# Own gate blocks of the second RG-LRU layer as three products of split parts, with the second parts made by GpSimd

## The chip, the core and the metric

One core of a Trainium2 chip runs the whole program. The time is the device time in microseconds (us) of one execution; a kernel's time is the median of several runs. The engines are TensorE (PE in the profile; PEld is its weight load), VectorE (DVE), ScalarE (ACT), GpSimd (POOL) and SyncE (SP), which here only issues DMAs. Each engine runs its own instructions in order and waits for others by semaphores.

## The reference

A trunk of four layers on 256 tokens of width 1024 in float32: an RG-LRU mixer, a gating mixer, a short convolution, and an RG-LRU mixer again, each followed by a squared-ReLU MLP. The change touches the last mixer, the second RG-LRU layer:

```python
gate, xr = jnp.split(h @ w_in, 2, axis=-1)          # 1024 -> 2 x 1280
gate = jax.nn.gelu(gate)
xr = _causal_dwconv(xr, conv_w) + conv_b            # 4 taps
xh = xr.reshape(b, s, A_HEADS, A_HEAD_DIM)          # 16 heads of 80
r  = sigmoid(einsum("bshi,hij->bshj", xh, gate_a_w) + gate_a_b)
ig = sigmoid(einsum("bshi,hij->bshj", xh, gate_x_w) + gate_x_b)
log_a = -LRU_C * r * softplus(-lam)
a = exp(log_a);  u = sqrt(-expm1(2 * log_a)) * (ig * xr)
hs = associative_scan(a, u)
return (hs * gate) @ w_out                          # 1280 -> 1024
```

## The kernel before

**Products.** TensorE computes most products of float32 values as three products of split parts: both operands are split into a rounded first part (type float32r) and the rest, and `mm3` (L251) adds first x first, first x second and second x first. Weights are split on the core: a chunk of 128 x 2048 arrives in two halves of 1024 columns (`raw`), ACT makes the first part of each half (`whi`, L187) and DVE the rest (`wlo`, L190). There are 12 raw buffers (`rawp`, L136) and five buffers each for `whi` and `wlo` (L137, L138). `next_chunk` (L236) keeps chunks asked for up to four ahead. SP issues each load as soon as a raw buffer is free.

**Gates.** The 1280 channels are ten tiles of 128 channels, in two groups of five. They are ordered so that four tiles of a group hold one whole head and part of another, and the fifth (the hub) the remaining parts. The gate matrices of a group are thus an own block of 128 x 128 for each of the five tiles and each of the two gates, four row strips from the hub to the others (L756) and four column strips back (L763). They come in two raw chunks of eight and six blocks, which are not split: `gate_steps` (L728) multiplies them as plain float32 (L748, L756, L763). A tile's products of both gates fill one PSUM bank of eight.

**Order of the work.** TensorE's instructions run in the order in which the program writes them. For the layer they are a generator (`tensor_steps`, L674) whose steps are mostly twelve products each. In this layer (`LRU_ORDER[1]`) steps 1 to 20 project the convolution branch (ten tiles), 21 to 24 are the first gates, 25 to 28 two gated tiles, 29 to 32 the second gates, 33 to 48 the other eight gated tiles, 49 to 68 the output projection, four steps for each pair of hidden tiles.

What the other engines do between is written out by hand in `LRU_STEPS[1]` (L73 to L77) and read by `run` (L646). `P` or `P2` lets the generator go on by one step or two. `C` is the next cast of a raw half on ACT, `S` the next split on DVE. Every other word is a method with a tile or pair number, and `in_order` (L203) ties each instruction behind the one before it on its engine, so the list is each engine's order. The words that matter here, by pair of tiles unless said:

- `ns`, `na`, `nv`: the row of the norm (ACT, TensorE, ACT and DVE).
- `x`: branch bank times that row (DVE, L794). `K`: last tap and bias (ACT, L802, two instructions). `k`: the other three taps (DVE, L808, six instructions). Their result is the tile pair `xc`.
- `wE`: loads ACT's table for the exponential (L869). `r` (by tile): both tanh of a tile's gates (ACT, L820), which frees its bank. `e`: decay terms (ACT, L832). `d`, `u`, `v`, `w`, `a`, `z`: the rest of the recurrence and the scan (DVE). `s`: square root (ACT, L846).
- `g`, `G`: gated bank times the row (DVE, L873), gelu (ACT, L877). `m`: scan times gate (DVE). `i`, `o`: the first and second part of the hidden pair for the output projection (ACT L885, DVE L890).

Of the kernel before, what the change touches and what calls it, by code (L numbers as in the profile page):

```python
# [9 lines left out]
F32 = mybir.dt.float32  # L10
F32R = mybir.dt.float32r
# [4 lines left out]
P = 128  # L16
T = 256
D = 1024
KD = D // P
# [7 lines left out]
CHUNK = 2048  # L27
# [25 lines left out]
LRU_ORDER = (  # L53
    (
        ("branch", 8), ("branch", 2), ("gated", 4), ("gates", 0),
        ("gates", 1), ("gated", 2), ("gated", 4),
    ),
    (
        ("branch", 4), ("branch", 2), ("branch", 4), ("gates", 0),
        ("gated", 2), ("gates", 1), ("gated", 4), ("gated", 4),  # L60
    ),
# [16 lines left out]
)  # L78


# [12 lines left out]
ROW_LAYERS = (1,)  # L93

UNSPLIT = None


def _const_columns():
# [15 lines left out]
def trunk(ctx: ExitStack, tc: tile.TileContext, xT, consts, sbias, first, weights, out, widths, whole, causal):  # L114
    nc = tc.nc
    MULT, ADD, SUB, MAX = ALU.mult, ALU.add, ALU.subtract, ALU.max
# [7 lines left out]
    def pool(name, n_bytes, at=None, bufs=1):  # L124


        nonlocal taken
        gap = 0 if at is None else (at - taken) % 1024
        if gap:
            ctx.enter_context(tc.tile_pool(name=f"before_{name}", bufs=1)).tile([P, gap // 4], F32, name=f"gap_{name}")  # L130
        taken += gap + n_bytes
        return ctx.enter_context(tc.tile_pool(name=name, bufs=bufs))
# [3 lines left out]
    rawp = pool("rawp", 12 * 4096, 0, bufs=12)  # L136
# [4 lines left out]
    def wtile(dtype=F32, name="wk"):  # L141
        return wide.tile([P, 2, T], dtype, name=name, tag="wk", bufs=N_WIDE)

    def bank():
        return psum.tile([P, 512], F32, name="ps", tag="ps")
# [4 lines left out]
    ready = {}  # L150
# [44 lines left out]
    used = [0]  # L195
# [24 lines left out]
    def ask():  # L220
        with tc.high_priority(offset=-LATER):
            for load, cast, split in fetch(asked[0]):
                load()
                casts.append(cast)
                splits.append(split)
            asked[0] += 1
            if not placed[0]:
                make_parts()

    def make_parts():  # L230
        while splits:
            if casts and len(casts) == len(splits):
                casts.pop(0)()
            splits.pop(0)()

    def next_chunk():  # L236
        i = used[0]
        used[0] += 1
        while asked[0] < n_chunks:
            ahead = sum(n not in whole for n in range(i + 1, asked[0]))  # L240
            if asked[0] > i and ahead + (asked[0] not in whole) > AHEAD:
                break
            ask()
        return ready.pop(i)
# [385 lines left out]
    class Mixer:  # L630


        def __init__(self, layer, nxt):
            self.layer = layer
            self.nxt = nxt
            self.added = False
            self.sq = {}
            self.scale = RowScale() if layer in ROW_LAYERS else Scales()
            self.banks = {"branch": [], "gated": [], "gates": {}}
            self.xr, self.xc, self.hs, self.gs, self.parts = {}, {}, {}, {}, {}  # L640
            self.rg, self.ig, self.qs, self.t = {}, {}, {}, {}
            self.acc = None
            self.in_order = chain()
            self.tensor = self.tensor_steps()
# [29 lines left out]
        def tensor_steps(self):  # L674
# [32 lines left out]
            for i in range(KR // 2):  # L707
                whole_pair = (self.layer, i) == UNSPLIT
                if whole_pair:
# [18 lines left out]
        def gate_steps(self, g):  # L728

            at, w = 0, None

            def block():
                nonlocal at, w
                if at % 8 == 0:
                    w = next_chunk().rearrange("p (k w) -> p k w", w=P)
                at += 1
                return w[:, (at - 1) % 8, :]

            hub = g * GRP + GRP - 1
            tiles = range(g * GRP, hub)
            banks = self.banks["gates"]

            for m in (*tiles, hub):
                banks[m] = bank().rearrange("p (j t) -> p j t", t=T)
                for e in range(2):
                    nc.tensor.matmul(banks[m][:, e, :], block(), self.tile_of(m), start=e == 0, stop=False,  # L748
                                     skip_group_check=True)
                if m in (tiles[1], hub):  # L750
                    yield
            for e in range(2):
                b = block()
                for i, m in enumerate(tiles):
                    q = slice(i * SHARE, (i + 1) * SHARE)
                    nc.tensor.matmul(banks[m][:, e, :], b[q], self.tile_of(hub)[q], start=False, stop=True,  # L756
                                     tile_position=(i * SHARE, 0), skip_group_check=True)
            yield
            for e in range(2):
                b = block()  # L760
                for i, m in enumerate(tiles):
                    q = slice(i * SHARE, (i + 1) * SHARE)
                    nc.tensor.matmul(banks[hub][q, e, :], b[:, q], self.tile_of(m), start=False, stop=True,  # L763
                                     tile_position=(0, i * SHARE), skip_group_check=True)
            yield
# [40 lines left out]
        def k(self, i):  # L806
            c, x = self.xc[i], self.xr[i]
            return [nc.vector.scalar_tensor_tensor(out=c[:, j, d:], in0=x[:, j, :T - d],  # L808
                                                   scalar=self.tap(3 - d, 2 * i + j), in1=c[:, j, d:],
                                                   op0=MULT, op1=ADD)  # L810
                    for d in (1, 2, 3) for j in range(2)]


        def r(self, m):
# [292 lines left out]
    for step in HEAD_STEPS.split():  # L1107
        what, i = step[0], int(step[1:] or 0)
# [39 lines left out]
def _out_chunks(w):  # L1148
    return [w[k:k + 2 * P].reshape(2, P, D).transpose(1, 0, 2).reshape(P, 2 * D) for k in range(0, w.shape[0], 2 * P)]
# [32 lines left out]
def _weight_chunks(p):  # L1182
# [7 lines left out]
    for i, kind in enumerate(KINDS):  # L1190
        j = counts[kind]
        counts[kind] += 1
        if kind == "a":
# [8 lines left out]
            for n, c in enumerate(_out_chunks(p["a_w_out"][j])):  # L1202
                out += unsplit([c[:, :D], c[:, D:]]) if (j, n) == UNSPLIT else [c]
        elif kind == "b":
# [63 lines left out]
```

## Time and profile before

| | |
|---|---|
| median of 3 runs | 1063.13 us (1063.07 to 1063.28) |
| the profiled execution | 1063.05 us, of which its span is 1061.3 us |
| PE, PEld busy | 1053.5 us (99%), 1041.9 us (98%) |
| DVE, ACT busy | 716.4 us (68%), 615.5 us (58%) |
| POOL busy | 27.2 us (3%) |
| granted clock of TensorE | 0.998 of full speed |

A row of the timeline has start and duration in us, the engine, the line, the operation, out<-in by the program's names (buffer numbers left out), shapes and count, and in brackets how long the engine stood idle before it and what ended that. Rows of equal instructions that follow each other are merged. A plain float32 product has two records on TensorE, so ten of them are "x20". In the second RG-LRU layer the branch projection ends and the first gates begin at 809.72 us, the second gates run from 821.75 to 828.14 us.

### The profile page before, as it was taken

The numbers are of one execution on the slowest core, as the hardware profiler recorded it, in microseconds if no ns is written. First come the engines' busy times: TensorE is split into PE (matmuls) and PEld (weight loads), VectorE is DVE, ScalarE is ACT, GpSimd is POOL, SyncE is SP. The second block draws the span as 40 slices with busy tenths as digits, with TensorE's granted clock in tenths as the row PEclk, the third lists the DMA queues.
The fourth block names the chain that finished last, engine by engine and source line by source line (L and its number), as shares of the span: only waits on it lengthen the run. The fifth ranks groups of instructions, "written<-read, shape, count | busy, mean of one in ns | idle before, by whom it ended". The sixth has DMA issues, their size and how long they took to land.

```text
span 1061.3 us, 21619 instructions
## 1 busy us (share of the span) xinstructions
PE 1053.5 (99%) x9138; PEld 1041.9 (98%) x9138; DVE 716.4 (68%) x921; ACT 615.5 (58%) x866; POOL 27.2 (3%) x75
## 2 busy tenths in 40 slices
PE   9999999999999999999999999999999999999997
PEld 9999999999899999999999999999999999999997
DVE  7999965565758754545797764455589899655553
ACT  7798644454664754445554574446556977544442
POOL 2400000000110000000000000000000000000000
PEclk9999999999999999999999999999999999999999
DMA  9655676555556566555475466555645546755301
GB/s 339 254 236 179 235 262 199 196 188 197 196 170 207 189 208 200 196 187 185 153 237 196 159 228 206 190 191 179 196 152 180 186 149 222 259 197 191 129 1 40
DMA packets 58417, 203.39 MB, mean 192 GB/s; under 512 B 6608, under 2 KB 7760, under 8 KB 58320
## 3 DMA queue, kind: packets, MB, share of 16 engines
q1 hardware_dynamic: 58176, 201.75, 56.2%
q8 instruction: 71, 1.16, 0.4%
q10 hardware_dynamic: 144, 0.26, 0.1%
q14 instruction: 26, 0.21, 0.1%
HBM read 200.94 MB, written 1.05 MB: 190 GB/s over the span
## 4 chain that ended last, share of the span: by engine, by line
PE 99%; DVE 0%; DVEq 0%; issue 0%
PE ps L253 92%; PE ps L937 2%; PE ps L748 2%; PE ps L699 1%; PE ps L756 0%; PE ps L259 0%; PE ps L763 0%; PE ps L973 0%; PE ps L695 0%; PE ps L1047 0%; PE ps L1054 0%; PE ps L393 0%; DVE o L1071 0%; PE ps L337 0%; DVEq L1264 0%; PE ps L422 0%
## 5 line engine op out<-in xcount | busy, mean ns | idle before, releaser
L190 DVE TENSOR_TENSOR wlo<-raw,whi 128x1024 fp32r<-128x1024 f32 (+1 forms) x379 | 442.9, 1199 | 225.9 <-ACT whi L187 225.9
L253 PE MATMUL ps<-xs,whi 128*128 128x256 f32 x3120 | 533.3, 276 | 0.0
L187 ACT CAST whi<-raw 128x1024 fp32r<-128x1024 f32 (+1 forms) x379 | 375.7, 1030 | 266.7 <-issue 153.4
L253 PEld LDWEIGHTS ps<-xs,whi 128*128 128x128 f32 x3120 | 469.9, 188 | 1.3 <-issue 0.4
L253 PE MATMUL ps<-xs,wlo 128*128 128x256 f32 x1560 | 430.7, 276 | 0.0
L253 PE MATMUL ps<-lo,whi 128*128 128x256 f32 x1312 | 362.2, 276 | 0.0
L253 PE MATMUL ps<-hi,wlo 128*128 128x256 f32 x1312 | 362.1, 276 | 0.0
L253 PE MATMUL ps<-hi,whi 128*128 128x256 f32 x1312 | 362.1, 276 | 0.0
L253 PEld LDWEIGHTS ps<-xs,wlo 128*128 128x128 f32 x1560 | 292.9, 188 | 0.0
L253 PEld LDWEIGHTS ps<-lo,whi 128*128 128x128 f32 x1312 | 246.3, 188 | 0.1
L253 PEld LDWEIGHTS ps<-hi,whi 128*128 128x128 f32 x1312 | 246.3, 188 | 0.0
L253 PEld LDWEIGHTS ps<-hi,wlo 128*128 128x128 f32 x1312 | 246.3, 188 | 0.0
L530 DVE TENSOR_TENSOR lo<-hsq,hi 128x512 fp32r<-128x512 f32 x64 | 44.0, 688 | 52.6 <-ACT hsq L528 51.3
L527 ACT ACTIVATE hi<-u 128x512 fp32r<-128x512 f32 x64 | 40.3, 630 | 24.3 <-DVE u L526 23.8
L291 ACT ACTIVATE xs<-x,cst 128x256 fp32r<-128x256 f32 x64 | 29.2, 502 | 31.1 <-DVE x L478 28.6
L524 ACT ACTIVATE u<-ps 128x512 f32<-128x512 f32 x32 | 18.9, 592 | 48.2 <-PE ps L253 48.2
L528 ACT ACTIVATE hsq<-u 128x512 f32<-128x512 f32 x64 | 39.5, 617 | 0.0
L295 DVE SCALAR_TENSOR_TENSOR xs<-x,cst,xs 128x256 fp32r<-128x256 f32 x64 | 28.6, 482 | 8.4 <-ACT xs L291 8.4
L526 DVE SCALAR_TENSOR_TENSOR u<-ps,rs 128x512 f32<-128x512 f32 x32 | 22.0, 687 | 16.8 <-PE ps L253 16.6
L808 DVE SCALAR_TENSOR_TENSOR xc<-xr,cst,xc 128x255 f32<-128x255 f32 (+2 forms) x60 | 24.1, 475 | 0.0
L315 DVE TENSOR_TENSOR sum<-sum,sq 128x256 f32<-128x256 f32 x52 | 21.9, 420 | 1.3 <-ACT sq L496 0.6
L937 PE MATMUL ps<-whi,xs 128*128 128x512 f32 x64 | 20.5, 394 | 0.0
(150 smaller groups left out, 479.4 us busy)
## 6 DMA issues: line engine op xcount, KB each, us to landing
raw<-weights SPq DMA_DIRECT2D x369, 512.0 KB, 4.2
raw<-first SPq DMA_DIRECT2D x16, 256.0 KB, 4.3
raw<-weights SPq DMA_DIRECT2D x4, 384.0 KB, 6.6
x<-xT SPq DMA_DIRECT2D x8, 128.0 KB, 4.0
out<-o SPq DMA_DIRECT2D x3, 256.0 KB, 2.7
sb<-sbias SPq DMA_DIRECT2D x2, 256.0 KB, 5.3
out<-o ACTq DMA_DIRECT2D x1, 256.0 KB, 3.4
cst<-consts SPq DMA_DIRECT2D x1, 128.0 KB, 6.5
```

The lines of the kernel that those rows point to most:

```text
L187: return nc.scalar.copy(out=hi[:, s], in_=raw[:, e])
L190: return nc.vector.tensor_tensor(out=lo[:, s], in0=raw[:, e], in1=hi.bitcast(F32)[:, s], op=SUB)
L253: nc.tensor.matmul(ps, a, b, start=start and n == 0, stop=stop and n == 2, skip_group_check=True)
L291: return nc.scalar.activation(xs_now[k][0], x_res[k // 2][:, k % 2, :], AF.Copy, scale=col(g_name, g_at + k))
L295: return nc.vector.scalar_tensor_tensor(out=lo, in0=x_res[k // 2][:, k % 2, :], scalar=col(g_name, g_at + k), in1=hi.bitcast(F32), op0=MUL ...
L315: return [nc.vector.tensor_tensor(out=sq_now[0], in0=sq_now[0], in1=sq[:, j, :], op=ADD) for j in range(2)]
L526: yield nc.vector.scalar_tensor_tensor(out=u, in0=ps, scalar=0.0, in1=both(scale.row), op0=MAX, op1=MULT)
L527: yield nc.scalar.activation(hi, u, AF.Square)
L528: yield nc.scalar.activation(sq, u, AF.Square)
L530: yield nc.vector.tensor_tensor(out=lo, in0=sq, in1=hi.bitcast(F32), op=SUB)
L808: return [nc.vector.scalar_tensor_tensor(out=c[:, j, d:], in0=x[:, j, :T - d], scalar=self.tap(3 - d, 2 * i + j), in1=c[:, j, d:], op0=MUL ...
L937: nc.tensor.matmul(ps[c], xs[a][:, s], b[:, k, :], start=kk == 0 and n == 0, stop=kk == KD - 1 and n == 2)
```

## The change

In the second RG-LRU layer (`SPLIT_GATES = (1,)`), the own blocks of the four tiles beside the hub are multiplied as three products of split parts. The hub's own blocks and all strips stay plain products. New steps make the parts:

- `W` casts the first gate chunk (eight blocks, 1024 columns) on ACT into a buffer `ghi`, and `V` makes the second part `glo` on GpSimd. Both buffers come from the 12 of `rawp`. `W` waits until the chunk has been asked for.
- `B` casts one or two tiles of `xc` on ACT into `xh`, and `N` makes the second parts `xl` on GpSimd. `B0.1` stands for tiles 0 and 1; group 0 takes `B0.1`, `B2.3`, group 1 `B5`, `B6.7`, `B8`.

The generator has as many steps as before: the first step of a group now holds all products with `xh` (16), the second those with `xl` (8) and the hub's two plain ones. The list of steps changes up to `r3`; from there it is the same.

```diff
-    "P4 C P C P ns S C S P na nv S C P S x0 x1 K0 K1 P2 C P S C k0 P S C x2 K2 k1 P S C P k2 P S P wE P C P C P2 "
-    "x3 x4 K3 K4 S k3 P P k4 P2 r3 r1 P r0 P C S P S e0 P u0 P g0 r2 C u1 P d0 e1 S r4 P d1 C P r8 S P r9 C u4 P "
+    "P4 C P C P ns S C S P na nv C P x0 x1 K0 K1 W0 V0 P2 C P k0 P x2 K2 k1 B0.1 N0.1 C S P S B2.3 N2.3 C P S k2 "
+    "C B5 N5 P S P C wE W1 V1 P C P C S P2 x3 x4 K3 K4 S k3 P P B6.7 N6.7 k4 P B8 N8 S P r3 r1 P r0 P C S P S e0 "
+    "P u0 P g0 r2 C u1 P d0 e1 S r4 P d1 C P r8 S P r9 C u4 P e4 S P2 d4 P s0 s1 v0 P v1 w0 G0 a0 P w1 r5 z0 C P "
...
@@ gate_steps
-            for m in (*tiles, hub):
+            split = self.layer in SPLIT_GATES
+            if split:
+                next_chunk()
+                at = 8
+                for m in tiles:
+                    banks[m] = bank().rearrange("p (j t) -> p j t", t=T)
+                for part, x in enumerate((self.xh, self.xl)):
+                    for i, m in enumerate(tiles):
+                        for e in range(2):
+                            for n, w in enumerate(self.gw[g][:2 - part]):
+                                nc.tensor.matmul(banks[m][:, e, :], w[:, 2 * i + e, :], x[m],
+                                                 start=e == 0 and part == 0 and n == 0, stop=False,
+                                                 skip_group_check=True)
+                    if part == 0:
+                        yield
+            for m in (hub,) if split else (*tiles, hub):
@@ new steps
+        def W(self, g):
...
+            while i not in ready:
+                ask()
+            raw = ready[i]
+            hi = rawp.tile([P, 1024], F32R, name="ghi", tag="raw")
+            lo = rawp.tile([P, 1024], F32R, name="glo", tag="raw")
+            self.gw[g] = [t.rearrange("p (k w) -> p k w", w=P) for t in (hi, lo)]
+            self.gate_parts = (raw, hi, lo)
+            return nc.scalar.copy(out=hi, in_=raw)
+
+        def V(self, g):
+            raw, hi, lo = self.gate_parts
+            return nc.gpsimd.tensor_tensor(out=lo, in0=raw, in1=hi.bitcast(F32), op=SUB)
+
+        def B(self, *ms):
+            n = len(ms)
+            hi = self.xh_new = wtile(F32R, "xh")[:, :n, :]
...
+            return nc.scalar.copy(out=hi, in_=self.xc[ms[0] // 2][:, j:j + n, :])
+
+        def N(self, *ms):
+            n = len(ms)
+            lo = wtile(F32R, "xl")[:, :n, :]
...
+            return nc.gpsimd.tensor_tensor(out=lo, in0=self.xc[ms[0] // 2][:, j:j + n, :],
+                                           in1=self.xh_new.bitcast(F32), op=SUB)
```

Before `x3`, the new list has 11 `C` and 7 `S` where the old one has 10 and 8; up to `r3` both have 9 `S`.

More of the change, by code (lines that the diff above doesn't have):

```diff
@@ L95 @@
 UNSPLIT = None
+SPLIT_GATES = (1,)
 def _const_columns():
@@ L637, in __init__ @@
             self.sq = {}
+            self.first_chunk = used[0]
+            self.gw, self.xh, self.xl = {}, {}, {}
             self.scale = RowScale() if layer in ROW_LAYERS else Scales()
@@ L811, in k @@
                     for d in (1, 2, 3) for j in range(2)]
+        def W(self, g):
+            i = self.first_chunk
+            for what, arg in LRU_ORDER[self.layer]:
+                if what == "gates":
+                    if arg == g:
+                        break
+                    i += 2
+                else:
+                    i += arg * P * KD // CHUNK
+            while i not in ready:
[12 more added lines that the diff above has]
+            hi = self.xh_new = wtile(F32R, "xh")[:, :n, :]
+            j = ms[0] % 2
+            for d, m in enumerate(ms):
+                self.xh[m] = hi[:, d, :]
+            return nc.scalar.copy(out=hi, in_=self.xc[ms[0] // 2][:, j:j + n, :])
+        def N(self, *ms):
+            n = len(ms)
+            lo = wtile(F32R, "xl")[:, :n, :]
+            j = ms[0] % 2
+            for d, m in enumerate(ms):
+                self.xl[m] = lo[:, d, :]
+            return nc.gpsimd.tensor_tensor(out=lo, in0=self.xc[ms[0] // 2][:, j:j + n, :],
+                                           in1=self.xh_new.bitcast(F32), op=SUB)
         def r(self, m):
```

6 rows, old and new, of the table LRU_STEPS are left out of this document.

## The prediction

> **What bounds the kernel now.** I read the page first, then the chain of work in order of time around the second RG-LRU layer, then the timelines of ScalarE (ACT), VectorE (DVE), the DMA queue (SPq) and GpSimd (POOL) there.
>
> ```profile
> span 1061.3 us, 21619 instructions
> PE 99%; DVE 0%; DVEq 0%; issue 0%
> ```
>
> TensorE is the bound: 99% of the chain that ended last is PE. In the layer the chain has no piece that is not PE:
>
> ```profile
> 792.01 17.71 PE ps L253 x156
> 809.72 4.32 PE ps L748 x20
> ...
> 816.11 5.64 PE ps L253 x48
> ...
> 828.14 58.69 PE ps L253 x516
> ...
> 887.07 164.59 PE ps L253 x1452
> ```
>
> Columns: start, duration, engine and line, count. L748 is the own gate blocks (ten products a group, two records each), L253 the split products. So the change can gain on PE only what it takes out of L748, and it loses whatever its new waits put between PE's steps. One profiled execution took 1063.05 us against a median of 1063.13; its span is 1061.3, and what lies around the span I leave as it is. All sums below start from 1063.05. A difference under 0.2% (2.1 us) is about what a measurement of this kernel cannot tell from none.
>
> **What the products gain.** A plain product costs 4.32 / 10 = 0.432 us; a split one 164.59 / 1452 = 0.1134, three of them 0.340. The change swaps 4 tiles x 2 gates x 2 groups = 16 blocks: 16 x (0.432 - 0.340) = 1.47 us less on PE, 0.74 in each group. Bounds: each new product loads its own weights as every L253 product does, so I see no reason for another pitch. If nothing else happened: 1061.6.
>
> **What the step lists add to ACT.** These are the rows of the layer:
>
> ```profile
> 798.66 2.08 ACT L802 ACTIVATE xc<-xr,cst 128x256 f32<-128x256 f32 x4 [4.93 <-DVE xr L794]
> ...
> 809.13 1.28 ACT L869 ACT_TABLE_LOAD   x1
> ...
> 816.66 0.46 ACT L820 ACTIVATE rg<-ps,half_b 128x256 f32<-128x256 f32 x1
> ...
> 866.39 2.01 ACT L187 CAST whi<-raw 128x1024 fp32r<-128x1024 f32 x2 [0.74 <-PE ps L253]
> 868.31 0.61 ACT L885 CAST hi<-rg 128x512 fp32r<-128x512 f32 x1
> ...
> 871.83 2.00 ACT L187 CAST whi<-raw 128x1024 fp32r<-128x1024 f32 x2 [2.92 <-issue]
> ```
> ```profile
> 795.67 2.35 DVE L190 TENSOR_TENSOR wlo<-raw,whi 128x1024 fp32r<-128x1024 f32 x2
> 797.94 1.28 DVE L794 TENSOR_TENSOR xr<-ps,rs 128x512 f32<-128x512 f32 x2
> ...
> 816.29 4.81 DVE L808 SCALAR_TENSOR_TENSOR xc<-xr,cst,xc 128x255 f32<-128x255 f32 x12
> ...
> 857.51 0.69 DVE L890 TENSOR_TENSOR lo<-rg,hi 128x512 fp32r<-128x512 f32 x1
> ...
> 868.95 0.69 DVE L890 TENSOR_TENSOR lo<-rg,hi 128x512 fp32r<-128x512 f32 x1
> ```
>
> ACT gets W0, W1 (a 128x1024 cast each, 0.95 us at the pitch of the 2.00 us pair) and B0.1, B2.3, B6.7 (128x512 casts, 0.61 as L885 at 868.31, 0.53 at pitch) and B5, B8 (one tile each, 0.4 between that and half of it). The list also has one C more ahead of `x3` (11 against 10) and the same number after it. So from there on every C takes the raw half after the one it took before.
>
> *First wait: the last hidden tile behind one C too many.* A step P is 12 products, 1.36 us. P49 starts at 828.14 + 16 x 1.36 = 849.90, P65 at 871.67. The row at 871.83 is the cast of the chunk five after the one that P61 to P64 use: there are five `whi` buffers, so it stood idle 2.92 us and began 0.16 after P64 ended. Before, `i4` (868.31) and `o4` (868.95) lay ahead of that cast. In the changed list `C S C P m4 S P i4 o4` the second C is that cast, so `i4` queues behind a wait for P64, and P65 needs `i4` and `o4`. Price: 0.16 + 0.95 + 0.61 + 0.69 = 2.4 us of idle PE, whatever happened earlier. I find no cover for it.
>
> *Second wait: the gates' tanh behind the last convolution.* `B6.7` and `B8` stand ahead of `r3 r1 r0` on ACT and `B8` needs `k4`, while before `r3` (816.66) ran beside `k3 k4` (816.29 to 821.1). When does `k4` end? The two splits ahead of `x0 x1` are put off (2.27 at their pitch), so `x0` starts at 795.67, K0 at about 796.4, `k0` at 797.5. Behind it on DVE: k0 2.4 (half of the 4.81 at 816.29), x2 0.60, k1 2.4, three S 3.4, k2 2.4, to 808.7. Then ACT sets the time: B5 0.4, C 0.95, table 1.28 and `wE` 0.1, W1 0.95, two C 1.9, K3 1.0 (half of 2.08) end at 815.3, and `k3 k4` (4.81) at 820.1. `B8` 0.4: `r3` at 820.5, 3.85 later than before. ACT has no slack to win that back:
>
> ```profile
> 822.00:850.00 28.00, 28.00 (x244) 26.30 (x243) 24.92 (x36) 27.47 (x47) 0.00 (x0) 1.00 0.54 186
> ```
>
> The fourth busy figure is ACT's: 27.47 of 28 us. I let 0.6 of the 3.85 be absorbed, so the third hidden tile's `o2` (857.51) comes 3.2 later, at 861.4 with its 0.69. PE wants it at P57, 860.78 before, 859.3 with the gain: 2.1 us. I take 2.0, bounds 0 (if `k4` ends two us sooner) to 3.
>
> Sum so far: 1063.05 - 1.47 + 2.4 + 2.0 = 1066.0.
>
> *Third wait: a raw buffer for W0.* `ghi` and `glo` come from the 12 raw buffers that the weight stream uses.
>
> ```profile
> 796.95 0.33 SPq L184 DMA_DIRECT2D raw<-weights  x1
> ```
> ```profile
> 798.05 0.33 SPq L184 DMA_DIRECT2D raw<-weights  x1
> ```
> ```profile
> SPq L184 <- DVE wlo L190: 77.7, 22, 11.6
> ```
>
> Start, duration, queue and line; the last row is the queue's waits by what ended them (total, times, longest). The DMAs at 796.95 and 798.05 went out just as the two splits at 795.67 ended (796.9 and 798.0): a freed buffer is taken at once, all twelve are in use, and the queue's waits are all for a split. The change puts those two splits behind `k1`, so the first buffer to come free after `K1` does so at 797.5 + 2.4 + 0.6 + 2.4 + 1.2 = 804.1. W0, ready at 798.4, waits for that if the stream has taken every earlier one; queued behind it on ACT are a C, K2, B0.1 and so on to K3. K2 then starts at 806.0, and from there K2 1.0, B0.1 0.53, C 0.95, B2.3 0.53, two C 1.9, B5 0.4, C 0.95, `wE` and its table 1.4, W1 0.95, two C 1.9 and K3 1.0 end at 817.5; W1 waits for a buffer of its own, which I put at 0.7. So K3 ends at 818.2, 2.9 later, and `r3` starts at 823.4. This reaches PE in full: of eight PSUM banks the gates of the first group hold five and a gated bank one, so the second group finds two, and its third and fourth tile wait for those that `r3` and `r1` free. Price 2.9, bounds 0 and 4.
>
> Free in this change: POOL's queue (the same row has POOL at 0.00, so nothing else stands behind V and N), the chunk that W asks for (it has been fetched by then), the other moved splits (the half at 795.67 is first used at P25, 816.1), and the later DMAs (the transfer of 796.95 becomes 805 to 810, its cast is at 816).
>
> **What GpSimd costs.** The trace has no two-input operation of this width on POOL. Nearest rows:
>
> ```profile
> 265.57 1.10 POOL L1079 TENSOR_SCALAR_AFFINE_SELECT raw<-raw 128x1024 f32<-128x1024 f32 x1 [225.17 <-DMA raw<-weights]
> ...
> 285.16 1.13 POOL L321 TENSOR_SCALAR rc<-rc 128x2 int32<-128x2 int32 x1 [18.50 <-ACT rc L320]
> 286.38 0.19 POOL L324 TENSOR_TENSOR rc<-rc 128x2 f32<-128x2 f32 x1
> ```
> ```profile
> 266.42 2.46 DVE L190 TENSOR_TENSOR wlo<-raw,whi 128x1024 fp32r<-128x1024 f32 x2 [3.08 <-ACT whi L187]
> ...
> 283.89 2.35 DVE L190 TENSOR_TENSOR wlo<-raw,whi 128x1024 fp32r<-128x1024 f32 x2
> ```
>
> One input of 1024 columns takes 1.10, so V takes 1.1 to 2.2 and N half of that for two tiles; I take the upper end, one pass for each input. At that, V0 from about 806 ends by 809.7, where P21 begins: it is hidden, but only just. The second pair of rows shows contention: an operation on two numbers, else 0.19, took 1.13 at 285.16 and ended as the splits ended (286.24), and in the other order the splits at 266.42 took 2.46 instead of 2.35 where they met the end of the POOL operation. So the two engines shut each other out at least partly. I price that in the forecast at nothing and carry the rest as a rival. For the duration, the Trainium skill, "GPSIMD Engine Reference", section 3.1, gives 4497 ns for a two-input sum of 2048 columns; an estimate from that page for V is 2.25 us and the sum would stay the same. No run so far shows it.
>
> **Forecast.** 1063.05 - 1.47 + 2.4 + 2.0 + 2.9 = 1068.9 us.
>
> **The rivals.**
>
> *No wait reaches PE (the other side).* It needs a `whi` buffer for the extra C before P64 ends, and `o2` no more than 1.1 us later than before. For: PE had no idle piece in the layer, and `o4` was 2.0 us early. Against: the row at 871.83 shows that very cast waiting for P64. It gives 1061.6. It decides at P65: if PE's step there follows without a gap, this is it. Chance 0.07.
>
> *Only the last wait.* W0 has its buffer and `k4` ends by 818, so `r3` is less than 2 us late and P57 loses nothing: 1061.6 + 2.4 = 1064.0. For: DVE's own work up to `k4` sums to some 22 us from 795.7, which would end it at 817.5. Against: K3 waits on ACT. Chance 0.10.
>
> *No wait for a raw buffer.* 1066.0. For: the program's order of buffers is not in the trace of before, and W0's operands have long landed. Chance 0.25.
>
> *DVE shut out by GpSimd.* Every N and V blocks the convolutions for its whole time: V0, N0.1, N2.3 and N5 hold back `k2` and its followers by 2.2 + 1.1 + 1.1 + 0.55 = 4.95, of which 1.3 is the time that `B5` had to spare on ACT, and N6.7 holds back `k4` by 1.1: 4.7 us on top of 1068.9, 1073.6. For: the row at 285.16. Against: at 266.42 DVE lost 0.1 us only. Chance 0.23. The Trainium skill, "SBUF — State Buffer", section "Who interferes with whom", says that a DVE instruction with two SBUF inputs and a GpSimd instruction that reads SBUF shut each other out, the second to issue blocking fully; by that page the sum would be this rival's. The row at 285.16 agrees with it on POOL's side.
>
> **How the numbers follow.** Forecast 0.35, the rivals 0.07, 0.10, 0.25 and 0.23 as said. The likeliest is 1068.9. For eight in ten I leave out the first rival and the upper part of the last: 1063.8 to 1074.0, which takes in the bounds of the second and third wait. Faster by over 0.2% would need more than the products can give: 0.02. Within 0.2%: the rest of the first rival and the second, 0.16. Slower: 0.82.
>
> **What would show it.** In the changed profile: L748 down to 2 products a group and the split ones at 0.113 each (gain right); a piece in the chain at P65, DVE `lo` L890's successor released by ACT behind a cast that waited for PE (first wait); the first tanh at or after the end of `k4`, and a gap at P57 (second); W0's cast starting at the end of a split, near 804 rather than 798.4 (third); N and V at 0.55, 1.1 and 2.2 us, and convolutions of more than 0.48 us each beside them (last rival). A chain that is PE alone through the layer would make the forecast wrong altogether.

## The result, and the profile after

| | before | after |
|---|---|---|
| median | 1063.2 us (1063.07 to 1063.4, 4 runs) | 1075.91 us (1075.37 to 1076.27, 4 runs) |
| the profiled execution | 1063.05 us, span 1061.3 us | 1075.92 us, span 1073.8 us |

The ratio is 1.0119, with an interval of 1.0106 to 1.0131: slower by 12.7 us, where 5.9 were forecast, and outside the range. Two executions on record, one of the kernel before (beside e5 to e8) and one of e9, had a granted clock of 0.65 and took some 1520 us; nothing is compared with them.

The page of the kernel after: its span, and the chain of work that ended last by engine.

```profile
span 1073.8 us, 21666 instructions
PE 91%; DVE 4%; ACT 3%; issue 1%; POOL 1%; DVEq 0%; ACTq 0%
```

TensorE held 99% of the chain before and holds 91% now. Waits have come into it, and the chain in order of time shows where (start, duration, engine and what; lines of the kernel after: L829 `k`, L863 `B`, L871 `N`, L761 the split gate products, L769, L777, L784 the plain ones, L257 all other split products, L191 `C`, L194 `S`, L946 `i`):

```profile
818.54 2.81 DVE xc L829 x6
821.43 0.63 ACT xh L863
822.13 6.73 POOL xl L871
828.90 1.65 PE ps L761 x6
830.55 1.71 PE ps L769 x4
832.26 2.02 PE ps L777 x16
...
835.67 5.58 PE ps L257 x47
841.27 1.05 ACT whi L191
...
881.37 1.04 ACT whi L191
...
883.57 4.62 DVE wlo L194 x4
```

Before, everything between 816.11 and 887.07 was PE. Now the second gates hang on GpSimd's `N6.7` (6.73 us), and what comes behind hangs on two casts, at 841.27 and 881.37. TensorE's own rows show what it waited for (the bracket is the idle time ahead of an instruction and what ended it; it is counted from the modelled end of the product before, so that from start to start, beyond the usual pitch of 0.113 us, 0.17 more is lost):

```profile
820.88 0.28 PE L761 MATMUL ps<-xh,ghi 128*128 128x256 f32 x1
...
822.10 0.38 PE L761 MATMUL ps<-xh,ghi 128*128 128x256 f32 x1 [0.60 <-ACT xh L863]
...
824.60 0.42 PE L761 MATMUL ps<-xh,ghi 128*128 128x256 f32 x1 [1.76 <-ACT ig L881]
...
828.90 1.65 PE L761 MATMUL ps<-xl,ghi 128*128 128x256 f32 x6 [1.92 <-POOL xl L871]
...
835.60 0.51 PE L257 MATMUL ps<-xs,whi 128*128 128x256 f32 x2
```
```profile
869.49 0.38 PE L257 MATMUL ps<-hi,whi 128*128 128x256 f32 x1 [0.95 <-ACT hi L946]
```
```profile
882.98 0.38 PE L257 MATMUL ps<-hi,whi 128*128 128x256 f32 x1 [1.58 <-ACT hi L946]
```

The second gates take 835.60 - 820.88 = 14.72 us from start to start. Before they took 828.08 - 821.59 = 6.49 in the same rows, and 0.74 less should do: 9.0 are lost. The three waits (for `B6.7`'s xh, for a bank that the tanh of `r` frees, for `N6.7`'s xl) make 0.77 + 1.93 + 2.22 = 4.9 of it. The other 4.1 have no wait in front of them: the products simply run slowly. The sixteen of L777 take 2.02 us, from 832.26 to 834.28; in the chain of before they are L756:

```profile
826.07 1.08 PE ps L756 x16
```

The table by windows tells why (window, its length, busy time of PE, PEld, DVE, ACT and POOL, then the granted clock):

```profile
821.40:824.81 3.41, 1.05 (x6) 0.74 (x6) 3.41 (x8) 2.02 (x6) 2.68 (x1) 1.00 0.99 352
824.81:828.22 3.41, 2.17 (x10) 1.88 (x9) 3.41 (x5) 3.41 (x8) 3.41 (x1) 0.50 0.88 305
...
831.64:835.05 3.41, 3.41 (x26) 1.62 (x28) 2.27 (x3) 3.24 (x7) 0.00 (x0) 0.50 1.00 358
835.05:838.46 3.41, 3.41 (x36) 2.98 (x29) 1.78 (x2) 0.98 (x3) 0.00 (x0) 1.00 0.72 250
```

After the first window, in which PE was busy 1.05 of 3.41 us, TensorE's clock was granted at half for three windows of the same length (the one not shown has 0.50 too). At P57 (869.49) and P65 (882.98) PE waited for the first part of a hidden pair and, 0.83 and 0.73 us after, for its second; together it lost 1.82 and 2.36 us, and behind P65 another 1.1 in small pieces up to the next norm.

Now the cause of the waits at the gates, on VectorE and GpSimd (start, duration, engine and line):

```profile
800.32 5.10 DVE L829 SCALAR_TENSOR_TENSOR xc<-xr,cst,xc 128x255 f32<-128x255 f32 x6
...
808.75 3.48 DVE L829 SCALAR_TENSOR_TENSOR xc<-xr,cst,xc 128x255 f32<-128x255 f32 x6
...
818.54 5.17 DVE L829 SCALAR_TENSOR_TENSOR xc<-xr,cst,xc 128x255 f32<-128x255 f32 x12 [1.72 <-ACT xc L823]
823.64 3.48 DVE L194 TENSOR_TENSOR wlo<-raw,whi 128x1024 fp32r<-128x1024 f32 x3
```
```profile
799.71 2.42 POOL L855 TENSOR_TENSOR glo<-raw,ghi 128x1024 fp32r<-128x1024 f32 x1 [492.14 <-ACT ghi L851]
802.16 1.40 POOL L871 TENSOR_TENSOR xl<-xc,xh 128x512 fp32r<-128x512 f32 x1
806.21 3.76 POOL L871 TENSOR_TENSOR xl<-xc,xh 128x512 fp32r<-128x512 f32 x1 [2.64 <-ACT xh L863]
...
822.13 7.41 POOL L871 TENSOR_TENSOR xl<-xc,xh 128x512 fp32r<-128x512 f32 x2 [3.03 <-ACT xh L863]
```

`k1` takes 5.10 us beside `V0` and `N0.1` where six such instructions alone take half of 4.81; `k2` takes 3.48 beside `N2.3`. GpSimd suffers in its turn: `N6.7` and `N8` take 7.41 while `k4`'s last parts and three splits run on without a loss (3.48 for three). The Trainium skill, "SBUF — State Buffer", section "Who interferes with whom", says that a VectorE instruction with two SBUF inputs contends with a GpSimd instruction that reads SBUF, by an exclusive lock, and that the order of issue decides who is blocked. The rows agree as far as the shutting out goes (5.10 against 2.4), but not on the order: `N6.7` stands from 822.13, and instructions that VectorE began later went ahead of it.

On ScalarE four rows answer to the prediction's waits: `W0`, the first tanh, and the two casts that PE hangs on.

```profile
798.60 1.04 ACT L851 CAST ghi<-raw 128x1024 fp32r<-128x1024 f32 x1
...
823.71 0.47 ACT L881 ACTIVATE rg<-ps,half_b 128x256 f32<-128x256 f32 x1
...
841.27 1.05 ACT L191 CAST whi<-raw 128x1024 fp32r<-128x1024 f32 x1 [4.68 <-PE ps L257]
```
```profile
881.37 1.04 ACT L191 CAST whi<-raw 128x1024 fp32r<-128x1024 f32 x1 [2.72 <-issue]
```

`W0` went out right behind `K1`. The first tanh stands at 823.71 (816.66 before), behind `B8`. The cast at 841.27 is the `C` in `r9 C u4`; ahead of it ScalarE stood still for 4.68 us, waiting for a product of PE, as a cast does when all five `whi` buffers are taken.

### The profile page after: what moved, and what is told of

It reads as the page before. It is cut to its first block, busy times and chain, and to the rows that moved or that the text cites. A ratio compares the mean times of both kernels' runs of the same rounds, so it can differ in the third digit from the quotient of the medians.

```text
span 1073.8 us, 21666 instructions
## 1 busy us (share of the span) xinstructions
PE 1058.8 (99%) x9154; PEld 1044.7 (97%) x9154; DVE 720.5 (67%) x921; ACT 619.5 (58%) x873; POOL 47.5 (4%) x82
## 3 DMA queue, kind: packets, MB, share of 16 engines
HBM read 200.94 MB, written 1.05 MB: 188 GB/s over the span
## 4 chain that ended last, share of the span: by engine, by line
PE 91%; DVE 4%; ACT 3%; issue 1%; POOL 1%; DVEq 0%; ACTq 0%
PE ps L257 85%; PE ps L998 2%; DVE xc L829 1%; DVE wlo L194 1%; PE ps L705 1%; PE ps L769 1%; ACT whi L191 1%; POOL xl L871 1%; PE ps L263 0%; PE ps L777 0%; PE ps L1034 0%; PE ps L784 0%; ACT q L893 0%; DVE xs L299 0%; ACT rg L893 0%
## 5 line engine op out<-in xcount | busy, mean ns | idle before, releaser
L194 DVE TENSOR_TENSOR wlo<-raw,whi 128x1024 fp32r<-128x1024 f32 (+1 forms) x379 | 442.8, 1199 | 222.6 <-ACT whi L191 222.5
L257 PE MATMUL ps<-xs,whi 128*128 128x256 f32 x3120 | 533.7, 276 | 0.2
L191 ACT CAST whi<-raw 128x1024 fp32r<-128x1024 f32 (+1 forms) x379 | 375.8, 1030 | 270.6 <-issue 153.0
L257 PEld LDWEIGHTS ps<-xs,whi 128*128 128x128 f32 x3120 | 470.0, 188 | 1.9 <-issue 0.8
L257 PE MATMUL ps<-xs,wlo 128*128 128x256 f32 x1560 | 430.7, 276 | 0.0
L257 PE MATMUL ps<-hi,whi 128*128 128x256 f32 x1312 | 362.4, 276 | 2.5 <-ACT hi L946 2.5
L257 PE MATMUL ps<-lo,whi 128*128 128x256 f32 x1312 | 362.5, 276 | 0.8 <-DVE lo L951 0.8
L257 PE MATMUL ps<-hi,wlo 128*128 128x256 f32 x1312 | 362.2, 276 | 0.0
L257 PEld LDWEIGHTS ps<-xs,wlo 128*128 128x128 f32 x1560 | 292.9, 188 | 0.0
L257 PEld LDWEIGHTS ps<-hi,whi 128*128 128x128 f32 x1312 | 246.3, 188 | 2.9 <-ACT hi L946 2.9
L257 PEld LDWEIGHTS ps<-lo,whi 128*128 128x128 f32 x1312 | 246.3, 188 | 1.2 <-DVE lo L951 1.2
L257 PEld LDWEIGHTS ps<-hi,wlo 128*128 128x128 f32 x1312 | 246.3, 188 | 0.0
L829 DVE SCALAR_TENSOR_TENSOR xc<-xr,cst,xc 128x255 f32<-128x255 f32 (+2 forms) x60 | 28.3, 541 | 1.8 <-ACT xc L823 1.7
L855 POOL TENSOR_TENSOR glo<-raw,ghi 128x1024 fp32r<-128x1024 f32 x2 | 5.3, 2662 | 493.2 <-ACT ghi L851 493.2
```

The lines of the kernel that those rows point to most:

```text
L191: return nc.scalar.copy(out=hi[:, s], in_=raw[:, e])
L194: return nc.vector.tensor_tensor(out=lo[:, s], in0=raw[:, e], in1=hi.bitcast(F32)[:, s], op=SUB)
L257: nc.tensor.matmul(ps, a, b, start=start and n == 0, stop=stop and n == 2, skip_group_check=True)
```

## The experiments

The theory: the early `C` causes the waits at P57 and P65 and what follows them, GpSimd's reads beside VectorE (with the tanh put behind `B6.7` and `B8`) those at the second gates, and the half clock multiplies both. The rivals: the late tanh is what P57 waits for (as predicted), the added casts fill ScalarE in any order, or the lists alone are at fault and GpSimd not. Unless said otherwise a time is one run, beside kernels before that took 1062.9 to 1063.2 us (e5 to e8 have none beside them to compare with). From run to run the program's first 45 us varied by up to 1.3 us; so where less matters, the stage is given, from the start of the second product of the norm ahead of the layer to that of the next norm (95.06 us before, 108.31 after).

### The cast one too early

**e1.** Only the second `C` ahead of `i4` is moved behind `o4`.

```diff
-    "... P C S C P m4 S P i4 o4 P S P ..."
+    "... P C S P m4 S P i4 o4 C P S P ..."
```

> The changed kernel with one edit at the end of the list: the second C of 'C S C P m4 S P i4 o4' goes behind o4. Theory (the extra C makes i4 wait for P64): the wait of 2.36 us at P65 shrinks to at most 0.5 (o4 is then behind one split), and the 1.1 us that PE waits for the next layer's xs and sums go with it, since four splits and the residual stand behind o4: 1075.9 - 3.0 = 1072.9 us, range 1072.3 to 1073.4. Rival (i4 is late because ACT's whole chain is late, the C does not matter): 1075.9.

1073.61 us. At P65 0.4 us is left of the wait, P57 keeps its 1.82, the pieces behind P65 stay too. So the first wait was what the prediction took it for, 2.0 us at P65. The half clock at the second gates lasted 6.8 us in place of 10.2, and they took 14.13 us in place of 14.72. The edit lies behind the gates and can't have done that: where the windows of the clock fall differs from run to run.

**e4.** The changed list with plain gate products: no `W`, `V`, `B`, `N`.

```diff
-SPLIT_GATES = (1,)
+SPLIT_GATES = ()
...
-    "... K0 K1 W0 V0 P2 ... k1 B0.1 N0.1 C S P ... k3 P P B6.7 N6.7 k4 P B8 N8 S P r3 r1 ..."
+    "... K0 K1 P2 ... k1 C S P ... k3 P P k4 P S P r3 r1 ..."
```

> The changed list of steps with plain products: no W, V, B, N, all own blocks plain as before. Theory: the convolutions and the first tanh are no later than before, so nothing is lost at the gates and at P57; the extra C still makes P65 wait 2.4 us and the 1.1 us behind it follow: 1063.05 + 3.5 = 1066.5 us. Rival (the re-timed list costs nothing by itself): 1063.1.

1070.38 us, stage 102.08 (+7.0). More than expected, and it tells what P57 waits for. On ScalarE:

```profile
816.26 0.47 ACT L881 ACTIVATE rg<-ps,half_b 128x256 f32<-128x256 f32 x1 [1.69 <-PE ps L777]
```
```profile
834.79 1.05 ACT L191 CAST whi<-raw 128x1024 fp32r<-128x1024 f32 x1 [4.66 <-PE ps L257]
```

The first tanh is as early as before (816.66), and yet P57 loses its 1.83 us. The idle 4.66 ahead of the cast of `r9 C u4` is all that is left to make ScalarE late. P57, P65 (2.37), 0.9 at the norm and one half-clock window behind P65 make up the 7.0.

**e5.** The changed kernel with that `C` put behind `o4`.

```diff
-    "... S P r9 C u4 P e4 ..."
+    "... S P r9 u4 P e4 ..."
...
-    "P m4 S P i4 o4 P S P ..."
+    "P m4 S P i4 o4 C P S P ..."
```

> The changed kernel with the C of r9 C u4 taken out and put behind o4. Theory (that one early C is what P57, P65 and the stage behind them wait for): the gaps at P57 (1.82 us) and P65 (2.36) and the 1.1 behind it go, 5.3 in all, so about 1070.6 us (1069.8 to 1071.4); the waits at the second gates (5.2) and the halved clock behind them stay. Rival (P57 waits because r3 is late): P57 keeps 1.8, so 1072.4. If neither reaches the end: 1075.9.

1069.48 us, 6.4 less; by the stage (101.49) it is 6.8, of which 5.4 lie behind the second gates. P57 and P65 have no gap, and of the pieces behind them 0.3 at the norm is left; the three waits at the second gates are as long as before (brackets 0.61, 1.77, 1.92), with two half-clock windows in place of three. That is worth the other 1.4 us, and it is not the edit's doing, which again lies behind the gates. The early `C` is shown as the cause of all but 0.3 us of what is lost behind the second gates.

### What GpSimd takes from VectorE

In these four the kernel before is left as it is, and GpSimd gets work whose result nobody reads, beside VectorE's busiest places.

**m1, m2, m3.** Set off by `x4`, beside `k3 k4`: four subtractions, twelve memsets, or eight copies, each of 128x512 (all begin with a copy of one column). The diff is m1's; in m2 the loop has `memset(out, 0.0)` twelve times, in m3 `tensor_copy(out=out, in_=self.xr[3])` eight times.

```diff
+        def q(self):
+            out = self.xr[1]
+            made = [nc.gpsimd.tensor_copy(out=out[:, 0, :1], in_=self.xr[4][:, 0, :1])]
+            for _ in range(4):
+                made.append(nc.gpsimd.tensor_tensor(out=out, in0=self.xr[3], in1=self.xr[4], op=SUB))
+            return made
...
-    "x3 x4 K3 K4 S k3 P P k4 P2 ..."
+    "x3 x4 q K3 K4 S k3 P P k4 P2 ..."
```

> The kernel before with four GpSimd subtractions of two inputs (128x512 each, into a tile that nobody reads any more) set off by x4, beside one split and k3 k4, which took 1.2 and 4.81 us. Theory (VectorE and GpSimd take turns at one port): k3 k4 take 7 to 9 us, and the four subtractions 2 to 4 us each where VectorE is busy, against 1.4 and less alone. Rival (the longer k1 of the changed kernel comes from its own inputs): 4.81 as before, 1.1 to 1.4 us each. The time says little: 1063 to 1066, as late convolutions hold back the second gates.

> The same with a copy of one column and twelve GpSimd memsets of 128x512 (about 0.47 us each) in place of the subtractions. Theory (it is reads that GpSimd and VectorE take turns at): k3 k4 stay at 4.8 us, the time at 1063. Rival (any GpSimd instruction holds VectorE back): 6 us or more.

> The kernel before with a copy of one column and eight GpSimd copies of 128x512 (one input) beside one split and k3 k4. Beside twelve memsets k3 k4 took 4.82 us, beside four subtractions ten of their twelve parts took 8.19. Theory (what holds VectorE back is what GpSimd reads, one pass for each input): the copies take about 0.7 us each, half of the subtraction's 1.43, and k3 k4 grow as long as they run, to 7 us or more. Rival (only a second input on GpSimd does it): k3 k4 stay at 4.8 to 5.0.

The times are 1063.83, 1062.68 and 1062.85 us. VectorE's `k3 k4` and GpSimd's work beside it, for m1, m2 and m3 in this order (4.81 us before):

```profile
816.13 8.98 DVE L815 SCALAR_TENSOR_TENSOR xc<-xr,cst,xc 128x255 f32<-128x255 f32 x12
```
```profile
816.34 5.73 POOL L801 TENSOR_TENSOR xr<-xr 128x512 f32<-128x512 f32 x4
```
```profile
816.76 4.82 DVE L815 SCALAR_TENSOR_TENSOR xc<-xr,cst,xc 128x255 f32<-128x255 f32 x12
```
```profile
816.95 6.96 POOL L801 MEMSET xr<- 128x512 f32 x12
```
```profile
816.12 7.65 DVE L815 SCALAR_TENSOR_TENSOR xc<-xr,cst,xc 128x255 f32<-128x255 f32 x12
```
```profile
816.31 6.00 POOL L801 COPY xr<-xr 128x512 f32<-128x512 f32 x8
```

Four subtractions cost VectorE 8.98 - 4.81 = 4.17 us, 1.04 each; eight copies 2.84, 0.36 each; twelve memsets nothing. So what counts is what GpSimd reads, and one input is enough. The time is about what GpSimd's instruction needs by itself: a subtraction took 5.73 / 4 = 1.43 us, a copy 6.00 / 8 = 0.75, and about 0.4 of each is a part of `k` (4.81 / 12) that it stood behind. An estimate from m1 for a `V` (twice the columns) is 2.1 us taken from VectorE, while VectorE makes the same part itself in 1.21 (e8, below).

**m4, m5.** Two subtractions beside four splits, set off by `o4`; in m5 also two ahead of `k3`, and the results rounded to float32r, as `N`'s is.

```diff
+            out = self.rg[4]
+            return [nc.gpsimd.tensor_tensor(out=out, in0=out, in1=self.gs[4], op=SUB) for _ in range(2)]
...
-    "P m4 S P i4 o4 P S P ..."
+    "P m4 S P i4 o4 q P S P ..."
```

> The kernel before with two GpSimd subtractions of 128x512 (into a dead tile, read by nobody) set off by o4, beside the four splits of VectorE that follow it (4.63 us at 869.56 before). Beside k3 k4 a subtraction took 1.43 us and VectorE lost the time. Theory (against two-input instructions of VectorE that follow each other without a gap GpSimd is the one that waits): the splits stay near 4.6 us and the two subtractions take 5 us or more together. Rival (VectorE loses here as well): 2.9 us for the two, the splits take 6 or more.

> The kernel before with two GpSimd subtractions of 128x512 set off by x4 (beside one split and k3 k4) and two set off by o4 (beside four splits), all four with their result rounded to float32r as N's is, into tiles that nobody reads any more. With plain float32 results they got their turn behind the instruction that VectorE had just begun: 1.4 us each beside k, 2.2 beside splits, VectorE losing 1.05 to 1.1 for each. In the changed kernel N6.7 took 6.7 us while splits and convolutions ran on. Theory (the type does not matter, a read beside VectorE is served in turn, and N6.7's case is another): 1.4 and 2.2 us again, VectorE loses 2.1 in each place. Rival (a rounded result is served last): 3 us and more for each, VectorE loses nothing.

1064.38 and 1063.83 us. VectorE and GpSimd in m4 (the four splits took 4.63 before):

```profile
870.24 6.84 DVE L190 TENSOR_TENSOR wlo<-raw,whi 128x1024 fp32r<-128x1024 f32 x4
```
```profile
870.47 4.39 POOL L799 TENSOR_TENSOR rg<-rg,gate 128x512 f32<-128x512 f32 x2 [562.25 <-DVE lo L894]
```

The expectation that VectorE would win here falls: it loses 2.21 us, 1.1 for each subtraction, as beside `k`, and GpSimd takes 2.2 for each instead of 1.4. With rounded results it is the same (6.83 and 4.40). Why `N6.7` of the changed kernel was kept waiting through eight instructions of VectorE, when these had their turn behind one, is therefore open; it is neither the shape nor the type of the result.

### The second gates

**e2.** The second parts are set to zero by GpSimd, which reads nothing then; the result lacks these parts.

```diff
-            return nc.gpsimd.tensor_tensor(out=lo, in0=raw, in1=hi.bitcast(F32), op=SUB)
+            return nc.gpsimd.memset(lo.bitcast(F32), 0.0)
```

(the same in `N`)

> The changed kernel with V and N writing zeros instead of the second parts, so that GpSimd reads nothing and waits for nothing (the second parts are left out of the result). Theory (VectorE and GpSimd shut each other out where both read the on-chip memory): the convolutions go back to 2.45 us a pair, k4 ends near 820.1 instead of 823.7, the first tanh starts near 820.5, no product waits for xl, and the clock stays full; what is left is 2.0 at P57, 2.4 at P65 and 1.1 behind it: 1063.05 - 1.47 + 5.5 = 1067.1 us. Rival (the order of the list alone makes the second gates late): the waits of 0.77 and 1.92 us stay, 1070 or more.

1067.66 us. All waits at the gates are gone, and the half clock there; what is left is the early `C`'s. `k1` (shown) and `k2` are back at 2.44 and 2.45 us, with the same list, and the first tanh stands at 819.48:

```profile
800.02 2.44 DVE L829 SCALAR_TENSOR_TENSOR xc<-xr,cst,xc 128x255 f32<-128x255 f32 x6
```

A memset also needs no cast ahead of it and is over sooner than a subtraction, so e2 prices GpSimd's part as a whole, its own time and the shutting out together; m1 to m3 show the shutting out alone. The run also shows when the clock falls:

```profile
858.63:862.04 3.41, 2.01 (x15) 1.62 (x14) 3.41 (x6) 3.41 (x6) 0.00 (x0) 1.00 0.18 44
862.04:865.46 3.42, 3.42 (x32) 3.42 (x31) 3.42 (x5) 3.38 (x5) 0.00 (x0) 1.00 0.63 201
872.29:875.70 3.41, 1.69 (x12) 1.49 (x13) 2.05 (x3) 2.27 (x3) 0.00 (x0) 1.00 0.67 213
875.70:879.11 3.41, 3.41 (x19) 3.41 (x18) 3.41 (x4) 0.00 (x0) 0.00 (x0) 0.50 0.73 237
```

A window with 2.01 us of PE (the wait at P57) is followed by full clock, one with 1.69 (P65) by half.

**e3.** The three splits behind `k4` are put behind `u1`.

```diff
-    "... k4 P B8 N8 S P r3 r1 P r0 P C S P S e0 P u0 P g0 r2 C u1 P ..."
+    "... k4 P B8 N8 P r3 r1 P r0 P C P e0 P u0 P g0 r2 C u1 S S S P ..."
```

> The changed kernel with the three splits behind k4 moved behind u1, so that VectorE does not start a train of splits when N6.7 and N8 are due. Theory (N6.7 is starved by that train: it ended 1.8 us after it): N6.7 and N8 end by 825, the waits of 2.22 and 0.27 us for xl go. If the clock fell because of these waits it stays full: 1075.9 - 2.5 - 3.8 = 1069.6; if the 0.77 and 1.92 us before them are enough to lower it: 1073.4. Rival (N of two tiles takes that long by itself): 1075.9.

1072.32 us. The wait for xl is gone, those for xh and the bank are not; one half-clock window at the gates in place of three. With the splits away, `N6.7` and `N8` come in time: the splits had kept GpSimd from its turn.

**e6, e10.** Zeros as in e2 and the `C` moved as in e5; e10 also puts the tanh first.

```diff
-    "... k3 P P B6.7 N6.7 k4 P B8 N8 S P r3 r1 P r0 P C S P ..."
+    "... k3 P P k4 P S P r3 r1 B6.7 N6.7 P r0 B8 N8 P C S P ..."
```

> The changed kernel, the same C moved, and the second parts of gates and xc set to zero by GpSimd instead of worked out (the output lacks those parts). Theory (the early C and the two-input operations on GpSimd are the whole loss): nothing is left but the gain of the products, 1063.0 - 1.47 = 1061.5 (1061.0 to 1062.0). Rival (the products, the casts on ScalarE or the taken raw buffers cost something too): 1063.0 or more.

> e6_zeros_c (both second parts set to zero, which the output lacks, and the C moved) with r3 r1 ahead of B6.7 and r0 ahead of B8. In e6 the first tanh started 3.0 us later than before, and 1064.0 was 2.5 above what the products alone give. Theory (this is the second wait of the prediction, a late tanh that full engines carry on to the last steps): it goes, 1061.6 (1061.1 to 1062.3). Rival (the added casts on ScalarE, 3.1 us in all, come out in the end in whatever order they stand): 1063.3 or more.

1064.02 and 1063.01 us. In e6 no wait is left at the gates, but the first tanh starts at 819.65, 3.0 late. It comes out at the end of the layer: PE waits at P65, for the next layer's first operands and at the norm. The stage is 96.78 us, 3.2 over what the products alone give (95.06 - 1.47 = 93.59). With the tanh first (817.37) it is 95.35: 1.4 of that goes and 1.8 stays, so neither the theory nor the rival of e10 has it all: a late tanh costs, and the added casts on ScalarE probably do as well (the expectation puts them at 3.1 us; by the prediction's prices all of them are 2 x 0.95 + 3 x 0.53 + 2 x 0.4 = 4.3).

**e11.** The real second parts again, with the `C` of e5, the tanh of e10 and the splits of e3.

```diff
-    "... k3 P P B6.7 N6.7 k4 P B8 N8 S P r3 r1 P r0 P C S P S e0 P u0 P g0 r2 C u1 P ..."
+    "... k3 P P k4 P P r3 r1 B6.7 N6.7 P r0 B8 N8 P C P e0 P u0 P g0 r2 C u1 S S S P ..."
```

> e5_c_after_gates with r3 r1 ahead of B6.7, r0 ahead of B8, and the three splits behind k4 put behind u1: everything that the list can mend, with the second parts still made by GpSimd. e5 was 1069.5 with 5.2 us of waits at the second gates and a halved clock behind them. Theory (two of the three waits come from the order, the third from convolutions that GpSimd lengthens, k4 at 823.7): the waits for a bank and for xl go, 2 to 3 us stay for xh of the last tile, 1064.8 us (1063.8 to 1066.2). Rival (the order is the whole cause): 1062.5 or less. Rival (GpSimd's parts come too late in any order): 1067.5 or more.

1066.35 us, 0.15 above the expected range. The wait for a bank is gone; two for xh and one for xl stay (brackets 0.60, 0.57, 0.69), and no window is at half clock. So of e5's loss the order made about 3 us (stage 101.49 in e5, 98.54 here), and GpSimd's subtractions 3.2 more against e10 (95.35), where it only writes.

### Other versions

**e8.** The second parts made by VectorE, with a list written for it.

```diff
-            return nc.gpsimd.tensor_tensor(out=lo, in0=raw, in1=hi.bitcast(F32), op=SUB)
+            return nc.vector.tensor_tensor(out=lo, in0=raw, in1=hi.bitcast(F32), op=SUB)
...
-    "... k3 P P B6.7 N6.7 k4 P B8 N8 S P r3 r1 P r0 ..."
+    "... k3 P P k4 P P r3 r1 B6.7 N6.7 P r0 B8 S N8 P ..."
```

> Both groups split, the second parts made by VectorE instead of GpSimd, the list written anew for that: r3 r1 ahead of B6.7, the splits later, the two C not early. Theory (without GpSimd beside it VectorE has the time for the second parts): no wait reaches TensorE and the gain of the products is left, 1063.0 - 1.47 = 1061.5 (1061.0 to 1062.2). Rival (VectorE is full here, so that its 5.5 us of second parts come back as waits at the second gates or at a split): 1063 to 1066.

1066.28 us; the rival's case, but for another reason than a full VectorE. Its parts on VectorE, and casts on ScalarE:

```profile
802.59 1.21 DVE L855 TENSOR_TENSOR glo<-raw,ghi 128x1024 fp32r<-128x1024 f32 x1
803.73 0.68 DVE L871 TENSOR_TENSOR xl<-xc,xh 128x512 fp32r<-128x512 f32 x1
```
```profile
808.86 1.06 ACT L191 CAST whi<-raw 128x1024 fp32r<-128x1024 f32 x1 [1.03 <-DMA raw<-weights]
812.29 1.04 ACT L191 CAST whi<-raw 128x1024 fp32r<-128x1024 f32 x1 [2.38 <-DMA raw<-weights]
```

Casts waited 3.4 us for transfers, probably since two raw buffers were taken and the splits that free the others came later; `K3`, queued behind, was late, and so were `k3`, `k4` and the second gates. Whether a better list would win with VectorE's parts wasn't tried.

**e7, e9.** Only the first group is split, its second parts by GpSimd; the `C` is moved. e9 is the same kernel in eleven runs.

```diff
-            split = self.layer in SPLIT_GATES
+            split = self.layer in SPLIT_GATES and g == 0
```

(and `W1 V1 B5 N5 B6.7 N6.7 B8 N8` are taken out of the list)

> Only the first group's four own blocks are split, its second parts by GpSimd; the second group is plain, and the C is moved. Theory (the loss lies at the second group's gates, whose xl and tanh meet the last convolutions): half of the gain is left, 1063.0 - 0.74 = 1062.3 (1061.8 to 1062.8). Rival (the first group's GpSimd work delays the convolutions up to the second gates even so): 1064 or more, with a wait at P29 or later.

> e7_first_group again, timed: only the first group split, the C moved. Theory (the split of the first group is free of its own waits): 0.7 us under the kernel before, ratio 0.9993, up to 0.9988 as in its one look. Rival (the one look was a lucky one): ratio 1.0 or above.

1061.83 us in one run; the median of eleven is 1062.14 us against 1063.07 for the kernel before, ratio 0.9991 with an interval of 0.9981 to 1.0. The chain of e7:

```profile
809.60 2.72 PE ps L761 x24
812.32 0.86 PE ps L769 x4
...
820.90 4.32 PE ps L769 x20
```

It is PE alone through both gates. The own blocks of the first group take 2.72 + 0.86 = 3.58 us, those of the second, left plain, 4.32: 0.74 gained. Of this 0.32 is lost again at the next norm, whose second product waits for VectorE's `sums`, so that the stage is 0.42 shorter (94.64):

```profile
886.25 0.39 PE L397 MATMUL ps<-sums,ones_r 128*128 128x256 f32 x1 [0.15 <-DVE sums L387]
```

GpSimd makes `k1` and `k2` just as long here (5.10 and 3.48), but `k3` starts at 816.61, against 816.29 before: the first group's 4 us are covered by slack that VectorE had there. This version beats the changed kernel. Against the kernel before its median is 0.9 us lower, more than the trace accounts for, and the interval reaches 1.0: a gain is not shown by the times.

## Why the prediction was wrong

**What bounds the kernel** and **what the products gain** were right: 0.74 a group, as e7 measures it.

**The first wait** was right in cause and price: 2.36 us at P65 against 2.4, and it goes in e1. Missed was what follows: 1.1 us up to the next norm, and in e2, e3 and e4 a half-clock window.

**The second wait** had about the right price at P57 (1.82 against 2.0), by a wrong cause. The tanh was late indeed, by 7.05 us instead of 3.85. (With its third wait the prediction had it at 823.4, close to the 823.71 measured, but by luck: that wait did not happen, and GpSimd's reads took its place; without them, in e2, the tanh stood at 819.48, a microsecond ahead of the 820.5 worked out without the third wait.) But e4 has the tanh on time and loses the same 1.83. P57 hung on the extra `C` at `r9`, which waits for a `whi` buffer like the one at P65. The prediction looked for the effect of one cast too many only at the place where the list before had no slack at all, and not at every later `C` in between. Where the early `C` is gone, the late tanh does show (e6 against e10), as 1.4 us at the end of the layer.

**The third wait** did not happen: `W0` started at 798.60. The bet that all freed buffers would be gone by then was lost; no view of before showed it, and the rival without this wait had 0.25. In e8 the two buffers probably do cost something, at later casts.

**What GpSimd costs** is the step that failed: "I price that in the forecast at nothing". It is the largest term. At the second gates 9.0 us were lost, 4.9 in waits and 4.1 to the half clock, and with a GpSimd that reads nothing (e2) none of it is left, though the order of the list is the same. The rival that had it priced the longer `k`s at 4.7 us; `k1` grew by 2.7, `k2` by 1.0 and `k3 k4` by 0.4, but more reached PE, as neither the wait for `N6.7` nor the half clock was in that sum. `V0` itself took 2.42 us; the prediction had 2.2, an estimate from the Trainium skill, "GPSIMD Engine Reference", section 3.1, gives 2.25. The trace of before held the hint, the row at 285.16 (though the 0.19 it was compared with is of another line; a cleaner case is L326, 1.05 us beside splits at 23.22 and 0.19 elsewhere). It was set against one row where VectorE lost 0.1 us, but there GpSimd's operation had been all but over when the splits began. The rest of the mechanism stood in the list: with `r3 r1 r0` behind `B8`, whatever makes `k4` late makes the banks of the second gates late as well, and three splits behind `k4` stood in `N6.7`'s way.

**The clock** had no term at all. It was read as 1.00 in the windows of before and left there, though the sum put 7.3 us of waits into one layer.

By the stage the runs take the loss apart as follows: 108.31 us; 101.49 with the `C` moved (e5; 1.4 of this difference is the half-clock window less); 98.54 with the tanh first and the splits later (e11); 95.35 with a GpSimd that only writes (e10, whose splits stand as before); and 93.59 would be the products alone. The last 1.8 us were not taken apart further.

## What to carry to other kernels

Work given to GpSimd is not free of VectorE: cost it as time taken from VectorE, here 1.04 us for a subtraction of 512 columns, where VectorE itself takes 0.68 (e8), and look whether VectorE has slack at that very place (in the first group it had, in the second not). When a list moves a cast of the weight stream forward by one, follow every later cast up to the point where the old order is met again, since each then waits for a buffer one chunk too early, with all that is queued behind it. And where waits would take more than half of some 3.4 us of TensorE's time, add the half clock that may follow them.

## What was not expected of the hardware

- The clock fell by windows of 3.41 us. In this layer, over all runs, a window at full clock in which PE was busy for less than half of it (seven, with 1.05 to 1.69 us of 3.41) was followed by one at half clock, and one with 1.97 us or more was not; once at half clock, a window with 2.17 us was followed by another (as shown above); e11 had 2.35 us of waits at the gates and 2.15 us of PE in the emptiest window, and kept its clock. The Trainium skill, "TensorE: Matmul & The Clock Gate", Part 1, has a free-running window of that length and a fall after an idle one; the length agrees, but here a window half idle was enough.
- A GpSimd memset of 512 columns (0.58 us each in m2) cost VectorE nothing, a copy 0.36 us, a subtraction 1.04 to 1.1.
- GpSimd's `N6.7` waited for some 5 us while eight instructions of VectorE passed. It ended, at 828.85, 1.2 us after VectorE had come to `gate` (827.65), which has an input in PSUM. In m1 to m5 GpSimd never waited for more than one, and what makes the difference stays open.
